# Seven block products for eight in the two feed-forward matrices of a decoder trunk, on one core

## The chip, the core and the metric

The kernel runs on one core of a Trainium2 chip. The metric is the device time of the whole program in microseconds, the median of the runs. Beside the runs there is one execution taken by the hardware profiler; all rows below are from it. The engines are TensorE (PE; its weight loads are listed as PEld), VectorE (DVE), ScalarE (ACT), GpSimd (POOL) and SyncE (SP), which issues every DMA here.

## What is computed

Two layers of a decoder trunk on 1024 tokens of width 1024, all in float32. A layer is a token mixer (attention heads and state-space groups behind a common projection, then an output projection), a layer norm, and a feed-forward block of width 4096 with a squared ReLU, with another layer norm behind it:

```python
h = layer_norm(DEEPNORM_ALPHA * h + mix_out, ln1_g[l], ln1_b[l])
ff = jnp.square(jax.nn.relu(h @ w_ff1[l] + b_ff1[l])) @ w_ff2[l] + b_ff2[l]
h = layer_norm(DEEPNORM_ALPHA * h + ff, ln2_g[l], ln2_b[l])
```

## The kernel before, in words

**Precision.** A float32 matrix is split into a high and a low part, `hi` by a rounding copy on ScalarE and `lo = x - hi` by a subtraction (`split`, L205 to 207, normally on VectorE). A block product is then three matrix products, hi·hi, hi·lo and lo·hi, added up in PSUM. A matrix product (`mm`, L203) has a 128x128 stationary operand and 512 columns.

**Order of work.** The program is written as Python generators which are stepped in turn (`run`, from L1172); each step issues some instructions. A scheduler then sorts the instructions of every engine by the order of the program and by the time at which it reckons that they can start. Every engine, SyncE too, takes its own list strictly in order. SBUF is one pool of 50 pages of 128 x 4 KB (`Pages`, L96; a part set aside is a `Ring`, L118); a page is taken from the front of the free list, and who takes it waits until its last reader is done. PSUM has eight banks under five names (`mm` 2, `a` 2, `b` 2, `c` 1, `s` 1).

**Feed-forward.** The hidden width is cut into 16 chunks of 256, the tokens into two halves of 512. `ff1(c, h)` (L1059) computes 256 hidden columns of one half, transposed: for each of two blocks of 128, 24 products into one bank, then ReLU with bias and a square on ScalarE, a square on VectorE and the subtraction that gives the low part. `ff2(cs, tiles)` (L1079) multiplies a chunk with its 256 rows of the second matrix: for each token tile of 128 and each of two column halves 6 products, then VectorE adds the bank to the residual page `r[i]`. `ff_load` (L1046) loads the weights of a chunk (512 KB a page) and splits them. The activations never leave SBUF. `ff_ahead` (L1104) takes chunks on the first token half from the time on at which that half is through its first layer norm, while the output projection (`gen_out`, L926), the layer norm (`ln_tiles`, L972) and the transposes (`ln_turn`, L1020) of the second half go on. `ffn` (L1120) does the rest: one `ff1` unit and one `ff2` unit in turn, the last two chunks together, token tile by token tile (event 3), so that the layer norm of a tile (`done`) follows as soon as it is complete.

**Beside it.** In layer 0 the tables of the state space of layer 1 (`gen_tables`, L464, `ssm_tables`, L395) are made during `ffn`, one step of them behind each event, 25 steps: the preparation (L294), and for each of eight units three steps with a ring of three pages. A unit has four products of 512 elements and a memset on GpSimd, nine operations of 512 elements on VectorE, some small matrix products, and stores 1.5 MB. The layer norm's scale and bias are two GpSimd operations of 1024 elements for each token tile (L991, L992).

## Time and profile before

| | |
|---|---|
| median of 3 runs | 2573.41 us (2568.72 to 2579.18) |
| profiled execution, span from first to last instruction | 2578.3 us |
| TensorE busy | 2387.0 us, 93% |
| VectorE busy | 1686.2 us, 65% |
| ScalarE busy | 895.4 us, 35% |
| GpSimd busy | 672.9 us, 26% |
| DMA | 297.24 MB, 115 GB/s over the span |

The profiled execution has no time of its own beside its span; the span lies inside the range of the three runs. "Busy" of TensorE counts overlapping matrix products once. In a list of groups "xN" is the number of instructions and "mean ns of one" the time of one alone; matrix products overlap, so that one that takes 390 ns alone starts every 226 ns. Layer 0's feed-forward lies at about 520 to 1360 us of the span, layer 1's at 1780 to the end.

### The profile page before, as it was taken

The numbers are of one execution on the slowest core, as the hardware profiler recorded it, in microseconds if no ns is written. First come the engines' busy times: TensorE is split into PE (matmuls) and PEld (weight loads), VectorE is DVE, ScalarE is ACT, GpSimd is POOL, SyncE is SP. The second block draws the span as 40 slices with busy tenths as digits, with TensorE's granted clock in tenths as the row PEclk, the third lists the DMA queues.
The fourth block names the chain that finished last, engine by engine and source line by source line (L and its number), as shares of the span: only waits on it lengthen the run. The fifth ranks groups of instructions, "written<-read, shape, count | busy, mean of one in ns | idle before, by whom it ended". The sixth has DMA issues, their size and how long they took to land.

```text
span 2578.3 us, 30595 instructions
## 1 busy us (share of the span) xinstructions
PE 2387.0 (93%) x11200; PEld 1951.8 (76%) x11200; DVE 1686.2 (65%) x2967; ACT 895.4 (35%) x1416; POOL 672.9 (26%) x537
## 2 busy tenths in 40 slices
PE   8988787879999999999999998896999999999995
PEld 7766675657788888888878786784778888888884
DVE  8686687876676666545584667789685545454548
ACT  4444566341332322222232544745232212121221
POOL 3465566141111111000152546624030000000004
PEclk9998898979999999999999999997999999999998
DMA  6588873332232322212145768532322212121201
GB/s 217 203 276 250 225 193 102 102 114 74 66 99 92 119 79 86 85 47 76 36 128 182 237 198 253 159 91 90 121 67 66 82 33 66 33 66 33 82 17 66
DMA packets 156471, 297.24 MB, mean 115 GB/s; under 512 B 55456, under 2 KB 74016, under 8 KB 156320
## 3 DMA queue, kind: packets, MB, share of 16 engines
q1 hardware_dynamic: 156320, 295.29, 37.0%
q8 instruction: 88, 1.44, 0.2%
q14 instruction: 63, 0.52, 0.1%
HBM read 228.90 MB, written 63.96 MB: 114 GB/s over the span
## 4 chain that ended last, share of the span: by engine, by line
PE 66%; DVE 13%; DMA 7%; issue 3%; ACT 2%; POOL 1%; SPq 1%; DVEq 0%; ACTq 0%; POOLq 0%
PE ps_mm L203 37%; PE ps_a L203 12%; PE ps_b L203 11%; PE ps_s L203 2%; DMA vr<-vD 2%; DVE wl L188 2%; PE ps_c L203 2%; DMA K<-qk 1%; PE ps_b L764 1%; SPq L185 1%; DVE hT L188 1%; POOL qt L188 1%; DVE S L740 1%; DVE CY L506 1%; DMA wr<-in_w_in_dram 1%
## 5 line engine op out<-in xcount | busy, mean ns | idle before, releaser
L203 PE MATMUL ps_mm<-hT,wh 128*128 128x512 f32 x2816 | 892.6, 396 | 21.5 <-DVE qt L678 11.1
L203 PEld LDWEIGHTS ps_mm<-hT,wh 128*128 128x128 f32 x2816 | 531.4, 190 | 135.6 <-DVE qt L678 9.0
L203 PE MATMUL ps_mm<-hT,wl 128*128 128x512 f32 x1408 | 554.5, 394 | 0.3 <-DVE wl L188 0.3
L200 ACT ACTIVATE wh<-wr 128x1024 fp32r<-128x1024 f32 (+1 forms) x233 | 241.6, 1051 | 458.3 <-PE ps_a L203 257.1
L188 DVE TENSOR_TENSOR wl<-wr,wh 128x1024 fp32r<-128x1024 f32 (+1 forms) x233 | 312.8, 1354 | 105.2 <-ACT wh L200 104.8
L203 PEld LDWEIGHTS ps_mm<-hT,wl 128*128 128x128 f32 x1408 | 268.0, 190 | 56.7 <-DVE wl L188 0.7
L200 ACT ACTIVATE rl<-ps_mm,cols 128x512 f32<-128x512 f32 x128 | 88.1, 688 | 599.4 <-PE ps_mm L203 596.6
L203 PE MATMUL ps_a<-wh,H 128*128 128x512 f32 x928 | 288.1, 391 | 1.6 <-DVE r L188 1.6
L203 PE MATMUL ps_b<-wh,H 128*128 128x512 f32 x928 | 286.6, 389 | 0.0
L188 DVE TENSOR_TENSOR rl<-rl 128x512 f32<-128x512 f32 x128 | 108.5, 848 | 267.9 <-ACT rl L200 267.9
L188 DVE TENSOR_TENSOR r<-ps_a,r 128x512 f32<-128x512 f32 x216 | 148.6, 689 | 140.0 <-PE ps_a L203 140.0
L188 DVE TENSOR_TENSOR r<-ps_b,r 128x512 f32<-128x512 f32 x216 | 146.4, 687 | 100.6 <-PE ps_b L203 99.1
L203 PEld LDWEIGHTS ps_a<-wh,H 128*128 128x128 f32 x928 | 173.1, 188 | 38.5 <-DVE r L188 2.0
L203 PEld LDWEIGHTS ps_b<-wh,H 128*128 128x128 f32 x928 | 174.2, 188 | 36.2
L203 PE MATMUL ps_mm<-wh,ms 128*128 128x512 f32 x512 | 166.0, 406 | 19.4 <-ACT wh L200 17.0
L188 POOL TENSOR_TENSOR xm<-xm,AG 128x1024 f32<-128x1024 f32 x7 | 16.7, 2391 | 633.1 <-ACT xm L200 633.1
L188 POOL TENSOR_TENSOR r<-xh,AG 128x1024 f32<-128x1024 f32 x24 | 67.1, 2815 | 439.5 <-DVE xh L194 439.5
L203 PE MATMUL ps_a<-wl,H 128*128 128x512 f32 x464 | 180.8, 390 | 0.0
L203 PE MATMUL ps_b<-wl,H 128*128 128x512 f32 x464 | 180.7, 389 | 0.0
L194 POOL TENSOR_SCALAR S<-S,mn 128x384 f32<-128x384 f32 (+7 forms) x128 | 105.7, 829 | 137.9 <-DVE mn L743 82.8
L203 PEld LDWEIGHTS ps_mm<-wh,ms 128*128 128x128 f32 x512 | 96.7, 194 | 42.1 <-ACT wh L200 17.5
L200 ACT ACTIVATE S<-S,mn 128x384 f32<-128x384 f32 (+7 forms) x128 | 98.8, 772 | 78.1 <-DVE mn L740 71.4
(260 smaller groups left out, 3803.0 us busy)
## 6 DMA issues: line engine op xcount, KB each, us to landing
wr<-in_w_ff_dram SPq DMA_DIRECT2D x152, 512.0 KB
wr<-in_w_in_dram SPq DMA_DIRECT2D x40, 512.0 KB
cs<-cs SPq DMA_DIRECT2D x32, 512.0 KB
LV<-LV SPq DMA_DIRECT2D x32, 512.0 KB
DL<-DL SPq DMA_DIRECT2D x32, 512.0 KB
qk<-q SPq DMA_DIRECT2D x32, 512.0 KB
wr<-in_w_out_dram SPq DMA_DIRECT2D x32, 512.0 KB
K<-qk SPq DMA_DIRECT2D x64, 256.0 KB
```

Source lines behind the costliest of these rows:

```text
L185: return self.nc.sync.dma_start(out=out, in_=in_)
L188: (eng or self.nc.vector).tensor_tensor(out, x, y, op)
L194: (eng or self.nc.vector).tensor_scalar(out, x, s0, s1, op0, op1)
L200: self.nc.scalar.activation(out, x, f, **k)
L203: self.nc.tensor.matmul(out, lhsT, rhs, start=start, stop=stop, **k)
L506: nc.vector.tensor_tensor_scan(C[:, g], s["rho"][:, g0 + g:g0 + g + 1].to_broadcast([P, P]), A[:, g], 0.0, OP.mult, OP.add)
L740: nc.vector.tensor_tensor_reduce(pp[:, c0:c1], ps[:, :c1 - c0], self.mask[:, m0 + c0:m0 + c1], -0.125, mn[:, 0:1] if n else 3e38, OP.add, ...
L764: nc.tensor.transpose(pt[:, base:base + P], PP[i][:, P * j:P * j + P], self.ident)
```

## The change

Both matrices of the feed-forward are cut into quadrants and multiplied in Winograd's form of Strassen's scheme: seven block products for eight, with sums of the quadrants of both operands ahead of them (S1 to S4 on the activations, T1 to T4 on the weights) and sums of the products behind. The first matrix is done in two phases. Phase A (`gen_ffa`) has the two products of the first token half and runs where `ff_ahead` ran; what it gives (product M1 and the finished quadrant H11) goes to DRAM. Phase B (`gen_ffb`) has the other five; it computes the sums of the weights on GpSimd, finishes the hidden quadrants, forms the sums S1 to S4 for the second matrix, and stores six pieces of 128x512 per chunk. `gen_ff2` loads those and the weights back, takes the first 14 chunks in pairs with seven products for a pair, and adds the seven sums at the end. The last two chunks are multiplied as before (`ff2_tail`). The residual pages go to DRAM behind the first layer norm and come back ahead of the second matrix; the first half's activations `x` go to DRAM too and come back for the sums (`gen_sums`). The tables of layer 1 are stepped by phase B, one step at each of its two yields a chunk, and the rest behind it.

The parts of the diff that matter (`split` is as before; `pair_split` splits a page into two pages, `one_split` half a page into one):

```diff
- "kmax": 2,
+ "kmax": 6,
+ "fbw": 13, "fbt": 8, "f2r": 14, "f2o": 20,
...
+    def gen_sums(self, X):
...
+        for j in range(2):
+            a21, a22, a11, a12 = X[j], X[2 + j], Z[j], Z[2 + j]
+            s1 = pg.get((2, 512), name="xs")
+            self.tt(s1, a21, a22, OP.add)
+            F["S1"].append(self.pair_split(s1))
+            yield
+            self.tt(a21, a11, a21, OP.subtract, eng=gp)
+            F["S3"].append(self.pair_split(a21))
+            yield
+            self.tt(a11, s1, a11, OP.subtract)
+            F["S2"].append(self.pair_split(a11))
+            yield
+            pg.free(s1, a21)
+            F["A22"].append(self.pair_split(a22))
+            yield
+            self.tt(a12, a12, a11, OP.subtract, eng=gp)
+            F["S4"].append(self.pair_split(a12))
+            yield
...
+    def quad(self, ps, B, A, start, stop):
+        bh, bl = B
+        n = 0
+        for k in range(4):
+            ah, al = (z[:, k % 2] for z in A[k // 2])
+            for w, x in ((bh, ah), (bh, al), (bl, ah)):
+                self.mm(ps, w[:, k], x, start and n == 0, stop and n == 11, skip_group_check=True)
+                n += 1
...
+    def gen_ffa(self):
...
+        for c in range(n):
+            nxt = start(c + 1) if c + 1 < n else None
+            yield
+            t, ps = cur
+            w = W.pop(c)
+            self.quad(ps, [z[:, 4:8] for z in w], F["A12"], False, True)
+            ring.free(*w)
+            load(c + 2)
+            self.act(t[:, 1], ps, AF.Relu, bias=self.hbias(2 * c))
+            self.act(t[:, 1], t[:, 1], AF.Square)
...
+            self.dma(d, t)
...
+    def gen_ffb(self):
...
+        wr, tr = Ring(pg, PRM["fbw"]), Ring(pg, PRM["fbt"])
...
+        def prep(c):
+            m0, m1 = (wr.get((KD, P), name="wr") for _ in range(2))
+            self.dma(m0, a["w_ff1"][l, 2 * c])
+            self.dma(m1, a["w_ff1"][l, 2 * c + 1])
+            u, v = (wr.get((KD, P), name="wt") for _ in range(2))
...
+            self.tt(T1, B12, B11, OP.subtract, eng=gp)
+            self.tt(T3, B22, B12, OP.subtract, eng=gp)
+            x = self.pair_split(u, shape=(KD, P), pg=wr)
+            self.tt(T2, B22, T1, OP.subtract, eng=gp)
+            wr.free(u)
+            self.tt(T4, T2, B21, OP.subtract, eng=gp)
+            wr.free(m0)
+            y = self.pair_split(v, shape=(KD, P), pg=wr)
+            wr.free(v)
+            z = self.one_split(B22, shape=(2, 4, P), pg=wr)
...
+            p5 = self.psum(("mm", "a")[c % 2])
+            self.quad(p5, first(x), F["S1"], True, False)
+            self.act(M5, p5, AF.Copy)
+            p6 = self.psum("b")
+            self.quad(p6, first(y), F["S2"], True, False)
+            self.tt(U2, p6, M1, OP.add)
+            self.quad(p5, [z[:, 0], z[:, 1]], F["S4"], False, True)
...
+            self.tt(A12, p5, U2, OP.add)
+            self.relu_square(A12, self.hbias(2 * c + 1))
+            yield
+            self.quad(p6, last(x), F["S3"], False, True)
...
+            self.tt(U3, p6, M1, OP.add)
+            self.tt(A22, U3, M5, OP.add, eng=gp)
...
+            self.quad(p4, last(y), F["A22"], True, True)
...
+            self.tt(A21, U3, p4, OP.subtract)
+            self.relu_square(A21, self.hbias(2 * c))
...
+                self.tt(S1, A21, A22, OP.add)
+                self.tt(S3, H11, A21, OP.subtract)
+                self.dma(d[:, 1:3], u)
+                self.tt(S2, S1, H11, OP.subtract)
+                self.tt(S4, A12, S2, OP.subtract)
+                self.dma(d[:, 3:5], v)
+                self.dma(d[:, 0], A12)
+                self.dma(d[:, 5], A22)
...
+    def gen_ff2(self, r):
...
+        R, O = Ring(pg, PRM["f2r"]), Ring(pg, PRM["f2o"])
...
+            if g == 0:
+                G[0, c] = take(p0, gp, True), take(page(((0, ah[:, 1]), (1, hq[:, 0]))))
+            elif g == 1:
...
+                self.tt(u[:, 0], B12, B11, OP.subtract, eng=gp)
+                self.tt(u[:, 1], B22, B12, OP.subtract, eng=gp)
+                G[1, c] = take(u, gp, True), take(s)
+            else:
...
+                self.tt(v[:, 0], B22, u[:, 0], OP.subtract, eng=gp)
+                R.free(u)
+                self.tt(v[:, 1], v[:, 0], B21, OP.subtract, eng=gp)
...
+                b22 = self.one_split(B22, pg=O)
...
+                a22 = self.one_split(x[:, 0], pg=O)
...
+                G[2, c] = take(v, gp), take(s), b22, a22
...
+        def product(i, ops, fresh):
+            nonlocal turn
+            for t in range(4):
+                ps = self.psum(tags[turn % 2][t])
+                o = slice(P * t, P * t + P)
+                for q, ((ah, al), (bh, bl)) in enumerate(ops):
+                    for j, (x, w) in enumerate(((ah, bh), (ah, bl), (al, bh))):
+                        self.mm(ps, x[:, o], w, q == 0 and j == 0, q == len(ops) - 1 and j == 2)
+                at = place[i](t)
+                if fresh and i in (1, 6, 7):
+                    self.act(at, ps, AF.Copy)
+                else:
+                    self.tt(at, at, ps, OP.subtract if i == 4 else OP.add)
+            turn += 1
...
+        for t in range(4):
+            eng = gp if t % 2 else None
+            rt, rb, u2, u3 = r[t], r[4 + t], U[t][:, 1], place[7](t)
+            self.tt(rt[:, 0:512], rt[:, 0:512], U[t][:, 0], OP.add, eng=eng)
+            self.tt(u2, u2, U[t][:, 0], OP.add, eng=eng)
+            self.tt(rt[:, 512:1024], rt[:, 512:1024], rb[:, 512:1024], OP.add, eng=eng)
+            self.tt(rt[:, 512:1024], rt[:, 512:1024], u2, OP.add, eng=eng)
+            self.tt(u3, u3, u2, OP.add, eng=eng)
+            for c in (0, 512):
+                self.tt(rb[:, c:c + 512], rb[:, c:c + 512], u3, OP.add, eng=eng)
...
+            sums = self.gen_sums(X.pop(1))
+            for _ in sums:
+                next(side, None)
+            for _ in side:
+                pass
...
-            self.ffn(done, bg, final)
+            for _ in self.gen_ffb():
+                next(bg, None)
+            for _ in bg:
+                pass
+            for i in range(NT):
+                r[i] = pg.get(name="r")
+                self.dma(r[i], rS[i])
+            for _ in self.gen_ff2(r):
+                pass
+            final()
+            if not last:
+                self.wring = Ring(pg, 12)
+                self.proj_load()
+            for i in range(NT):
+                self.ff2_tail(i, r)
+                done(i)
```

In `gen_ff2` the products of a pair run in the order 1, 2, 5, 7, 6, 4, 3. `prep(1)` is issued ahead of product 1, `prep(2)` and the loads of the next pair ahead of product 5, `prep(0)` of the next pair ahead of product 6. U holds products 1 and 6, Y product 7; the others are added to `r` at once.

## Rows read from the trace of the kernel before

**Rows 1.** The page: span, and busy time of each engine
```profile
span 2578.3 us, 30595 instructions
PE 2387.0 (93%) x11200; PEld 1951.8 (76%) x11200; DVE 1686.2 (65%) x2967; ACT 895.4 (35%) x1416; POOL 672.9 (26%) x537
```

**Rows 2.** Busy time of each engine by stretch, granted clock, DMA
```profile
core 0: us, PE busy (x) PEld busy (x) DVE busy (x) ACT busy (x) POOL busy (x), PEclk, DMA share, GB/s
...
700.00:800.00 100.00, 100.00 (x445) 82.80 (x444) 72.85 (x160) 30.97 (x43) 14.88 (x22) 1.00 0.29 95
...
1500.00:1600.00 100.00, 90.11 (x492) 75.78 (x492) 71.02 (x145) 44.36 (x83) 60.14 (x55) 0.95 0.78 236
1600.00:1700.00 100.00, 90.23 (x481) 72.40 (x480) 81.13 (x186) 64.54 (x110) 56.73 (x53) 0.95 0.56 155
...
2200.00:2300.00 100.00, 100.00 (x443) 82.85 (x442) 46.70 (x64) 19.49 (x26) 0.00 (x0) 1.00 0.14 43
...
690.00:1300.00 610.00, 610.00 (x2784) 500.75 (x2783) 365.89 (x569) 156.99 (x230) 61.99 (x60) 1.00 0.25 81
```

**Rows 3.** Groups by line and form: TensorE, products with hT
```profile
L203 PE MATMUL ps_mm<-hT,wh 128*128 128x512 f32 x2816 | 892.6, 396 | 21.5 <-DVE qt L678 11.1 <-DVE r L197 4.0 <-DVE hT L188 3.1
L203 PE MATMUL ps_mm<-hT,wl 128*128 128x512 f32 x1408 | 554.5, 394 | 0.3 <-DVE wl L188 0.3
```

**Rows 4.** Timeline of VectorE at three places: start, duration, operation, count
```profile
520.71 7.40 DVE L188 TENSOR_TENSOR hT<-ht,hT 128x512 fp32r<-128x512 f32 x3 [3.24 <-ACT hT L200]
...
753.61 1.22 DVE L188 TENSOR_TENSOR wl<-wr,wh 128x1024 fp32r<-128x1024 f32 x1
754.74 0.28 DVE L188 TENSOR_TENSOR scr<-scr 128x128 f32<-128x128 f32 x1
...
756.95 0.68 DVE L188 TENSOR_TENSOR rl<-rl 128x512 f32<-128x512 f32 x1
757.55 0.68 DVE L188 TENSOR_TENSOR bst<-bst,tp 128x512 f32<-128x512 f32 x1
...
770.30 0.43 DVE L194 TENSOR_SCALAR cs<-wk 128x512 f32<-128x512 f32 x1
770.64 0.68 DVE L188 TENSOR_TENSOR r<-ps_a,r 128x512 f32<-128x512 f32 x1
```

**Rows 5.** Timeline of GpSimd beside the first of those places
```profile
519.65 2.34 POOL L188 TENSOR_TENSOR r<-r,AB 128x1024 f32<-128x1024 f32 x1
521.96 2.81 POOL L188 TENSOR_TENSOR r<-xh,AG 128x1024 f32<-128x1024 f32 x1
524.74 5.61 POOL L188 TENSOR_TENSOR r<-r,AB 128x1024 f32<-128x1024 f32 x2
```

**Rows 6.** One tile's operations: duration ns min/median/max, first and last start
```profile
L188 DVE TENSOR_TENSOR hT<-ht,hT x48: 670/681/2883, 520.7 to 1917.3; 128x512 fp32r<-128x512 f32 x48
...
L740 DVE CUSTOM_DVE_ANT_0 S<-ps_a,mask x128: 261/670/693, 156.6 to 1744.4; 128x512 f32<-128x512 f32 x80, 128x128 f32<-128x128 f32 x16, 128x256 f32<-128x256 f32 x16, 128x384 f32<-128x384 f32 x16
...
L188 POOL TENSOR_TENSOR AB<-AB x16: 1260/1286/1297, 239.8 to 1615.3; 128x512 f32<-128x512 f32 x16
```

**Rows 7.** The view of rows 2 for shorter stretches
```profile
500.00:670.00 170.00, 134.48 (x573) 106.60 (x573) 127.48 (x194) 56.67 (x76) 60.66 (x23) 0.89 0.24 78
...
550.00:560.00 10.00, 5.54 (x14) 4.43 (x15) 7.32 (x6) 4.01 (x4) 5.27 (x3) 0.52 0.64 210
1440.00:1450.00 10.00, 8.91 (x57) 6.94 (x56) 8.21 (x23) 4.33 (x11) 7.32 (x9) 1.00 0.94 333
```

**Rows 8.** The view of rows 3: ScalarE, a split of 1024 and a square of 512
```profile
L200 ACT ACTIVATE wh<-wr 128x1024 fp32r<-128x1024 f32 x231 | 240.3, 1055 | 456.3 <-PE ps_a L203 257.1 <-PE ps_mm L203 106.2 <-DMA wr<-in_w_ff_dram 40.9
...
L200 ACT ACTIVATE H<-rl 128x512 fp32r<-128x512 f32 x128 | 80.1, 627 | 1.8
```

**Rows 9.** Timeline of GpSimd: one product of the tables
```profile
765.75 1.10 POOL L188 TENSOR_TENSOR wk<-pw,bst 128x512 f32<-128x512 f32 x1
```

**Rows 10.** Who waited for whom: us in total, times, longest
```profile
POOL wk L188 <- DMA DL<-DL: 116.1, 6, 25.0
```

More of the change, by code (lines that the diff above doesn't have):

```diff
@@ L1038, in ln_turn @@
         pg.free(*XH)
-    def ff_begin(self, l, hT, r):
-        n = DFF // 256
-        self.F = dict(l=l, hT=hT, r=r, W={}, H={}, sums=None, next=False, last=n - 1, K=0,
-                      need=[(w, c) for c in range(n - 2) for w in (1, 2)])
-    def ff_load(self, lim=99):
-        F, ring, a = self.F, self.wring, self.a
-        while F["need"] and F["need"][0][1] <= lim and len(ring.free_list) >= 4:
-            w, c = F["need"].pop(0)
-            src, shape = (a["w_ff1"], (KD, P)) if w == 1 else (a["w_ff2"], (D,))
-            F["W"][w, c] = [self.load_w(src[F["l"], 2 * c + m], shape, pg=ring) for m in range(2)]
-        if not F["need"] and F["next"]:
-            self.proj_load()
@@ new lines, in pair_split, with one_split, x_turn @@
+    def pair_split(self, src, eng=None, shape=(2, 512), pg=None):
+        pg = pg or self.pg
+        hi, lo = (pg.get(shape, F32R, name="sp") for _ in range(2))
+        self.split(hi, lo, src, eng)
+        return hi, lo
+    def one_split(self, src, eng=None, shape=(2, 512), pg=None):
+        t = (pg or self.pg).get(shape, F32R, name="sh")
+        self.split(t[:, 0], t[:, 1], src, eng)
+        return t
+    def x_turn(self, h, XH, gcol, bcol, l, tags=("b",)):
+        pg = self.pg
+        cols = self.cols[l]
+        out = []
+        for k in range(KD):
+            pt = self.psum(tags[k % len(tags)])
+            for q in range(4):
+                self.nc.tensor.transpose(pt[:, q * P:q * P + P], XH[q][:, P * k:P * k + P], self.ident)
+            if k % 2 == 0:
+                out.append(pg.get((2, 512), name="xt"))
+            self.act(out[-1][:, k % 2], pt, AF.Identity, scale=cols[:, gcol + k:gcol + k + 1],
+                     bias=cols[:, bcol + k:bcol + k + 1])
+        pg.free(*XH)
+        return out
@@ new lines, in ff_begin @@
+    def ff_begin(self, l, X):
+        pg = self.pg
+        F = self.F = dict(l=l, n=DFF // 256, K=0, ah=[], hq=[], sums=None)
+        F["xD"] = []
+        A = []
+        for x in X:
+            d = self.dram.tile([P, 2, 512], F32, tag=f"xd{len(A)}", name=f"xd{len(A)}_{self.uid()}")
+            self.dma(d, x)
+            F["xD"].append(d)
+            A.append(self.pair_split(x))
+            pg.free(x)
+        F["A11"], F["A12"] = A[:2], A[2:]
+    def gen_sums(self, X):
+        pg, F = self.pg, self.F
+        gp = self.nc.gpsimd
+        Z = []
+        for d in F["xD"]:
+            z = pg.get((2, 512), name="xz")
+            self.dma(z, d)
+            Z.append(z)
+        for n in ("S1", "S2", "S3", "S4", "A22"):
+            F[n] = []
+        for j in range(2):
[16 more added lines that the diff above has]
+            yield
+            pg.free(a22, a11, a12)
@@ new lines, in ff2_tail @@
+    def ff2_tail(self, i, r):
+        F = self.F
+        o = slice((i % 4) * P, (i % 4) * P + P)
+        for n in range(2):
+            ns = slice(512 * n, 512 * n + 512)
+            ps = self.psum("ab"[(i + n) % 2])
+            q = 0
+            for W, X in F["tail"]:
+                (bh, bl), (ah, al) = W[n], X[i // 4]
+                for m in range(2):
+                    for x, w in ((ah, bh), (ah, bl), (al, bh)):
+                        self.mm(ps, x[:, m, o], w[:, m], q == 0, q == 11)
+                        q += 1
+            self.tt(r[i][:, ns], ps, r[i][:, ns], OP.add)
+            sums = F["sums"]
+            if sums is not None:
+                if n == 0:
+                    sums[i] = self.small("fst", [2, 6], bufs=4)
+                self.nc.vector.bn_stats(sums[i][:, n], r[i][:, ns])
+        if i % 4 == 3:
+            for _, X in F["tail"]:
+                self.pg.free(*X[i // 4])
+        if i == NT - 1:
+            for W, _ in F["tail"]:
+                for w in W:
+                    self.pg.free(*w)
@@ L1227, in run @@
             self.F = None
-            hT1 = [[None, None] for _ in range(KD)]
+            X = {}
+            rS = [self.dram.tile([P, D], F32, tag=f"rs{i}", name=f"rS{i}_{l}") for i in range(NT)]
             def gen_side():
@@ L1257, in gen_side @@
                 self.wring = Ring(pg, 8)
[L1258 to L1259 removed]
+                self.ff_begin(l, X.pop(0))
+                yield from self.gen_ffa()
             def out_ssm(h):
@@ L1321, in run @@
                     next(side, None)
-            while "F" not in st and self.F is None:
+            while self.F is None:
                 next(side)
@@ L1352, in run @@
                 self.proj_begin(l + 1, items(l + 1))
-                self.F["next"] = True
                 def final():
```

299 lines of the change are left out of this document (183 added, 116 removed).

## The prediction

> **What bounds the kernel now.** I read the page's first two parts first, then the busy time by 100 us stretches, then the groups of instructions, and last the timeline of VectorE and GpSimd where they work together. TensorE is busy 93% of a span of 2578.3 us [rows 1]. The windows tell where the other 7% lies: in the feed-forward stretches (690 to 1300 us in layer 0; 2200 to 2300 stands for layer 1) it is busy without a gap at the full clock of 2.4 GHz; in the latter 443 products of 128x512 start, so 100/443 = 0.2257 us each [rows 2]; in the mixer stretches VectorE and GpSimd are both at 55 to 80% and TensorE at 90% [rows 2]. So the feed-forward is bound by the number of matrix products and by nothing else, and a product removed there is worth 0.2257 us, as long as the other engines keep up with what replaces it. That is the question of this case. In that last stretch GpSimd does nothing and VectorE works 47% of the time [rows 2].
>
> **What is removed.** Before, a chunk of 256 hidden columns takes 2x2x24 = 96 products in the first matrix and 8x2x6 = 96 in the second; 16 chunks and 2 layers make 6144. The trace has them: 4224 products of hT, of which 1152 are the projections' q, k and u (48 outputs of 24), leave 3072 [rows 3]; the second matrix has as many. After, the first matrix takes 24 in phase A and 60 in phase B, 84 in a chunk. The second takes 7 products x 24 for each pair of chunks times 7 pairs, and the last two chunks stay as they were (192): 1368 for 1536. So 192 + 168 = 360 products a layer go, 720 in all: **-162.5 us**. Nothing else on TensorE changes by more than a few products.
>
> **What the other engines get.** Prices, from start to start where the trace has two in a row: VectorE 0.60 us for 512 elements and 1.13 for 1024 [rows 4]; GpSimd 1.27 for 512 and 2.34 for 1024 when left alone [rows 5, 6].
>
> The rows that speak against the change are those where both work. While GpSimd ran four 1024-element sums back to back, three VectorE operations on 512 elements took 7.40 us instead of 1.8, and the sums 2.81 instead of 2.34 [rows 4, 5]: one goes, then the other, 2.80 us for a couple that would need 2.34 + 0.60 = 2.94 strictly in turn. The same form ranges from 670 to 2883 ns; an operation with one operand in PSUM never passes 693 ns in 128, all of them in the attention, where GpSimd is busy [rows 6]. The evictions of the new kernel are of that kind. So two engines share something that VectorE needs only for two SBUF operands, and I add up both engines' times on it. The Trainium skill (SBUF — State Buffer, "SBUF: two separate sides") calls this an exclusive lock held for the whole instruction, against VectorE operations with two SBUF inputs; the trace agrees in kind, and in size it shows 5% of overlap where the page allows none. By the page, layer 0's phase B below would come to 276 us instead of 265, and the sum to 11 us more.
>
> *Phase A* (24 products, 5.4 us a chunk): one split of 1024 on ScalarE and VectorE, three 512 activations. No bound. Its 384 products (87 us) fill the stretch in which the second half's output projection, layer norm and operand sums go on; before, chunks of the first half did this. Both kernels start it at the end of attention. The stretch has 35.5 us of idle TensorE now (134.5 busy of 170, 500 to 670 us), with holes like the one at 550 to 560 [rows 7]. The change takes two VectorE operations per output off it and adds the sums: 14 VectorE operations of 1024 (16 us) and 4 of GpSimd (9.4 us) that share the port, 25 us, behind the last transpose. Fill and chain are about equally long (130 to 140 us each), so something shows: **+12 us** for both layers, bounds -20 (all VectorE relief is gained) and +50 (all of the sums are exposed).
>
> *Phase B* (60 products, 13.5 us a chunk). VectorE: two lo splits of 1024 and one of 512, four evictions, four sums: 7.7 us. GpSimd: five sums, 6.35 us. Shared: 5.3 + 6.35 = 11.6 of 13.5 us. ScalarE: two splits near 1 us, one half, a copy, six activations near 0.6 [rows 8]: about 7. DMA: 1.5 MB in, 1.5 MB out, 3.15 MB in 13.5 us = 233 GB/s; the trace moves 333 GB/s at 94% of the DMA engines [rows 7], so it fits. The raw pages are free as soon as the chunk before is split, so loads go a chunk ahead. Layer 1: VectorE at about 72% with its waits, GpSimd at 47%. The nearest rows are 700 to 800 us (73% and 15%: TensorE 100%) and 1500 to 1600 (71% and 60%: 90%) [rows 2]; I take 96%, **+9 us** (0 to +22).
>
> In layer 0 the state-space tables of layer 1 run beside it, one step at each of phase B's yields, so eight units over some 12 chunks. A unit is four GpSimd products near 1.1 us [rows 9] and nine VectorE operations, seven of 0.60 and two scalar ones of 0.34 [rows 4]: 4.9 us. Shared time of the whole phase: GpSimd 16x6.35 + 8x4.4 + 6 = 143, VectorE 16x5.3 + 8x4.9 + 9 = 133 (the 6 and 9 are my allowance for the preparation, whose operations are small): 276 us, times 2.80/2.94 for the overlap = 265. TensorE has 16x13.5, and with an allowance of 9 for the tables' small products 225. So **+40 us**. Lower bound 0 (table work slips into gaps and off the chain); upper +91 (VectorE's 173 us of work there plus a wait for each of GpSimd's operations, 143, is 316). I stand at the shared time since the rows show a strict alternation.
>
> *Second matrix* (168 products, 37.9 us a pair). VectorE: 28 evictions (16.8), six lo splits of 1024, four of 512: 26.0 us. GpSimd: six lo splits of weights (2.35) and eight sums (1.27): 24.3. Shared: 9.2 + 24.3 = 33.5 of 37.9. With GpSimd at work 64% of the time a VectorE operation that needs the port waits some 0.6 us, ten of them 6 us: VectorE at 32 of 37.9, 85%. The nearest row is 1600 to 1700 us (81% and 57%): TensorE 90% [rows 2]. There attention's chains add waits that are not here; the operands here come two products ahead. I take 95.5%: 12 us a layer, **+24** (0 to +77, the second rival).
>
> *Phase B to the second matrix.* The splits of the first pair need pages that chunk 15 holds until its result is stored: after the last product an eviction 0.7, two activations 1.2, a store of 0.79 MB (2.4 at the 333 GB/s of rows 7), then the split on ScalarE 1.0 and GpSimd 2.35: 8 us idle. After such a hole the trace shows the clock at 0.52, the lower of its two levels (1.2 GHz), and 14 products in 5.5 us instead of 3.2 [rows 7]: 3 us more. Twice 11: **+22** (0 to +40). The eight r pages are reloaded on pages long free; first needed by product 2's eviction.
>
> *Second matrix to the last two chunks.* Seven sums for each of four tiles, half on VectorE (14x0.60), half on GpSimd (14x1.27) in strict dependence, before r can take the last evictions. r[0]'s seven take 4.2 us alone and 13 in turn with GpSimd's (7 x 1.87); r[3] is done after 18 us alone, 26 in turn; TensorE can run two tiles (10.8 us) ahead and reaches the fourth after 16. I take 8 a layer, **+16** (0 to +36). The last eight pages of operands (4.2 MB, 12.6 us at 333 GB/s) are loaded during the last three products (16.3 us).
>
> *SP's queue.* All new transfers (ah, hq, rS, xd) stand in one order with the loads. In phase B chunk c's last store waits for S4, some 3 us into the next chunk, and behind it stand the loads for chunk c+2, which have a whole chunk (13.5 us) until they are split: nothing, as long as no store is later than that.
>
> **Sum:** -162.5 + 12 + 9 + 40 + 24 + 22 + 16 = -39.5 us on the profiled 2578.3, which lies 4.9 us above the median of 2573.4 and inside the three runs' 2568.7 to 2579.2. From the median: 2573.4 - 39.5 = 2534; I say **2535**.
>
> **Rivals.** *All hidden.* If table work and waits fit in gaps, only the boundaries cost: -162.5 + 12 + 22 + 16 = -112, 2461. For it: on VectorE alone every phase is under 90%. Against: both stretches of rows 2 with GpSimd above 55% have TensorE at 90%.
>
> *The shared port decides everywhere (slower).* If each of the ten VectorE operations waits for a whole GpSimd operation (24.3/14 = 1.74 us), a pair takes 26.0 + 17.4 = 43.4 us: +5.5 x 14 = +77; layer 0's phase B +91. Sum -162.5 + 77 + 91 + 9 + 12 + 22 + 16 = +64, 2638. It decides from a mean wait of (37.9 - 26.0)/10 = 1.2 us on. For it: 2.5 us per operation in rows 4. Against: there GpSimd's queue never ran dry.
>
> *Tables hold GpSimd's queue.* They have three pages; now GpSimd waits up to 25 us for a table's store, 116 us in six waits [rows 10], which costs nothing since nothing is behind it. In phase B the next chunk's weight sums are behind it. If each of eight units blocks 5 us beyond the shared time, layer 0 loses 40 more: no change, 2574. Against: the scheduler reckons with a page's wait when it orders the queue.
>
> That the products are not removed is excluded by the counts above.
>
> **How the numbers follow.** Forecast 0.47 (2500 to 2560), all hidden 0.18, tables' queue 0.12, port everywhere 0.23. A change within 0.5% (2560.5 to 2586.3) is about what the measurement can't tell from none. Faster: 0.18 + nearly all of 0.47 = 0.63; same: the queue's 0.12 and 0.02 of the forecast's edge = 0.14; slower 0.23. These chances have both signs, so the likeliest's own range is 2500 to 2560; the range for 8 in 10 takes the better half of each far rival: 2452 to 2625.
>
> **What would show it.** 10480 instructions on TensorE for 11200. In layer 0's phase B (some 265 us) VectorE's two-SBUF operations at 1 to 3 us and TensorE near 85%; in layer 1's TensorE near 96%; in the second matrix 39 to 40 us a pair; an idle of 5 to 10 us at its start, with the low clock behind. Wrong if TensorE idles for DMA in phase B, if the pair takes over 42 us, or if layer 0's phase B is as quick as layer 1's.

## The result and the profile after

| | before | after |
|---|---|---|
| median (lowest to highest), 4 runs each | 2575.0 us (2568.7 to 2579.2) | 2602.2 us (2596.9 to 2607.8) |
| profiled execution, span | 2578.3 us | 2595.1 us (2596.9 as a run) |

The ratio is 1.0112, with an interval of 1.0089 to 1.0134: the change makes the kernel 1.1% slower, where 1.5% faster was forecast. The time lies inside the range of 2452 to 2625, on the slower side, which had a chance of 0.23.

The page of the kernel after, for [rows 1]:

```profile
span 2595.1 us, 31080 instructions
...
PE 2278.6 (88%) x10480; PEld 1835.9 (71%) x10480; DVE 1926.1 (74%) x3035; ACT 1125.5 (43%) x1716; POOL 1392.6 (54%) x937
```

The 720 products are gone. TensorE is busy 108 us less, yet the span is 17 us longer: TensorE now idles where it did not. The busy time by stage shows where; columns as in [rows 2] (layer 0: phase B, hand-over to the second matrix, second matrix; then the same for layer 1, and its end):

```profile
700.00:960.00 260.00, 232.47 (x1017) 181.75 (x1016) 220.15 (x303) 126.80 (x200) 152.65 (x119) 0.96 0.67 231
960.00:1045.00 85.00, 42.58 (x187) 31.97 (x186) 37.23 (x37) 27.30 (x43) 41.45 (x28) 0.72 0.51 180
...
1045.00:1285.00 240.00, 236.30 (x1037) 194.13 (x1037) 204.07 (x236) 91.84 (x107) 177.36 (x87) 1.00 0.46 150
1990.00:2220.00 230.00, 218.04 (x926) 176.07 (x924) 136.40 (x161) 104.99 (x154) 107.43 (x76) 0.98 0.66 228
2220.00:2245.00 25.00, 12.49 (x44) 9.54 (x44) 11.35 (x10) 12.63 (x16) 24.61 (x14) 0.80 0.78 267
2247.00:2500.00 253.00, 252.54 (x1113) 208.45 (x1112) 213.77 (x246) 97.02 (x115) 178.05 (x88) 1.00 0.43 136
2500.00:2595.00 95.00, 57.07 (x223) 44.15 (x221) 86.94 (x172) 11.66 (x10) 49.68 (x25) 0.83 0.14 55
```

In words, stage by stage. The second matrix runs almost without a gap in both layers, with VectorE at 85%; in layer 1 it takes 253/1113 = 0.2273 us a product, 38.2 us a pair. Phase B loses a little in layer 1 and more in layer 0. The hand-over of layer 0 is the surprise: 42 of 85 us idle, the clock at 0.72 in the mean, and no other engine is half busy either.

What those engines wait for is seen in GpSimd's and TensorE's timelines there (start, duration, idle before and its releaser):

```profile
992.87 1.04 POOL L189 TENSOR_TENSOR wk<-cst,fh 128x512 f32<-128x512 f32 x1
...
1008.71 1.10 POOL L189 TENSOR_TENSOR DL<-pw,spc 128x512 f32<-128x512 f32 x1 [0.18 <-DMA cs<-cs]
...
1022.84 1.04 POOL L189 TENSOR_TENSOR wk<-cst,fh 128x512 f32<-128x512 f32 x1 [12.57 <-DMA DL<-DL]
...
1033.66 1.10 POOL L189 TENSOR_TENSOR DL<-pw,spc 128x512 f32<-128x512 f32 x1 [8.72 <-DMA cs<-cs]
```

```profile
1010.59 0.56 PE L204 MATMUL ps_s<-DL,bst 128*16 128x112 f32 x2 [5.61 <-DVE DL L189]
...
1026.75 1.09 PE L436 MATMUL ps_s<-cst,wk 128*128 128x128 f32 x4 [14.32 <-DVE wk L189]
...
1035.54 0.55 PE L204 MATMUL ps_s<-DL,bst 128*16 128x112 f32 x2 [6.23 <-DVE DL L189]
...
1037.31 2.62 PE L204 MATMUL ps_b<-sp,sp 128*128 128x512 f32 x6
```

These are the last two units of the tables of layer 1. GpSimd waits for the store of a table page (DL, cs) before it may write the next one, as in [rows 10]; the small products of those units stand in TensorE's list ahead of the second matrix, and TensorE waits 26 us for them in the first three lines shown. Another 13 us are waits for the first pair's operands, as in layer 1 (5.8 us until 976 us, 7.5 until 987). In the kernel before, the first GpSimd operation of the eight units (first and last start at the end of the line) is this:

```profile
L188 POOL TENSOR_TENSOR wk<-cst,fh x8: 1039/1040/1528, 764.8 to 1023.4; 128x512 f32<-128x512 f32 x8
```

The last unit began at the same time, 1023 us, but there 340 us of feed-forward were still to come.

Where the time went, by stage: the loss of a stage is TensorE's idle time plus its busy time times what the granted clock lacks of full speed, added up over windows of 5 us. "Measured" is the loss after minus the loss before, rounded.

| stage, both layers unless said | forecast | measured |
|---|---|---|
| mixers and phase A | +12 | -2 |
| phase B, layer 0 | +40 | +36 |
| phase B, layer 1 | +9 | +16 |
| phase B to second matrix, layer 0 | +11 | +50 |
| phase B to second matrix, layer 1 | +11 | +16 |
| second matrix | +24 | +4 |
| its sums and the end of the layer | +16 | +38 |
| TensorE's busy time at the granted clock | -162.5 | -141.5 |
| sum | -39.5 | +16.8 |

### The profile page after: what moved, and what is told of

The parts are those of the page before. It is cut to its first block, busy times and chain, and to the rows that moved or that the text cites. A ratio compares the mean times of both kernels' runs of the same rounds, so it can differ in the third digit from the quotient of the medians.

```text
span 2595.1 us, 31080 instructions
## 1 busy us (share of the span) xinstructions
PE 2278.6 (88%) x10480; PEld 1835.9 (71%) x10480; DVE 1926.1 (74%) x3035; ACT 1125.5 (43%) x1716; POOL 1392.6 (54%) x937
## 5 line engine op out<-in xcount | busy, mean ns | idle before, releaser
L204 PE MATMUL ps_b<-sp,sp 128*128 128x512 f32 x1368 | 345.9, 400 | 23.1 <-DVE tu L189 9.7
L204 PEld LDWEIGHTS ps_b<-sp,sp 128*128 128x128 f32 x1368 | 261.2, 193 | 88.1 <-DVE tu L189 13.3
L204 PE MATMUL ps_a<-sp,sp 128*128 128x512 f32 x1008 | 257.1, 403 | 20.9 <-DVE r L189 12.4
L204 PE MATMUL ps_mm<-hT,wh 128*128 128x512 f32 x768 | 249.8, 403 | 9.9 <-DVE qt L679 8.1
L204 PEld LDWEIGHTS ps_a<-sp,sp 128*128 128x128 f32 x1008 | 195.6, 195 | 67.1 <-DVE r L189 15.0
L204 PE MATMUL ps_mm<-sp,sp 128*128 128x512 f32 x816 | 206.1, 398 | 33.1 <-ACT sp L201 16.1
L204 PEld LDWEIGHTS ps_mm<-sp,sp 128*128 128x128 f32 x816 | 155.2, 192 | 70.9 <-ACT sp L201 18.4
L204 PE MATMUL ps_mm<-sp,wh 128*128 128x512 f32 x512 | 175.5, 426 | 22.9 <-ACT mh L201 10.7
L204 PEld LDWEIGHTS ps_mm<-hT,wh 128*128 128x128 f32 x768 | 144.9, 192 | 42.0 <-DVE qt L679 8.2
L204 PE MATMUL ps_mm<-hT,wl 128*128 128x512 f32 x384 | 153.1, 399 | 0.9 <-DVE wl L189 0.9
```

The source lines that it names most:

```text
L204: self.nc.tensor.matmul(out, lhsT, rhs, start=start, stop=stop, **k)
```

## The experiments

Times are medians against the kernel before on the same chip (2574.9 to 2576.3 in the five comparisons); the changed kernel's is 2602.2. "Phase B" is the time from the first chunk's copy of M5 (the product of S1 and T1, which ScalarE copies out of PSUM) to the last's, 15 chunks, whose 900 products alone take 900 x 0.2257 = 203.1 us; "layer 0's rest" is from there to the last split of the layer's output. These come from one profiled execution each; the runs of one kernel lie up to 18 us apart, so a difference of a few us between two kernels tells nothing by itself.

**Runs 1 and 2: without layer 1's tables.**

```diff
-                bg = self.gen_tables(l + 1, 3)
+                bg = iter(())
+                self.sp[l + 1] = self.sp[l]
```

> The changed kernel without the tables of layer 1 (layer 1 reads layer 0's tables, so its output is that of other state-space parameters; the work of reading and using them is the same). Theory: the tables are what turns layer 0: they share GpSimd, VectorE and TensorE's queue with phase B, and their last units run alone behind it. Then phase B of layer 0 becomes like that of layer 1 (idle and slow-clock loss 44 to about 18 us) and the 42 us hole at its end becomes like the 14 us of layer 1: 54 us less, about 2548. Rival: phase B and the hand-over cost this by themselves (weights, stores, page reuse): at most 15 us less, 2587 or more.

> The kernel before without the tables of layer 1. Theory: there they lie wholly under TensorE's products, so it stays within 5 us of the 2575 of before. Rival: they cost the old kernel something too, 15 us or more less; then what the first run shows is not the change's alone.

Measured: 2524.3 us, 78 less than the changed kernel, and 2563.1, 12.7 less than before. So the tables cost 65 us more beside the new feed-forward than beside the old, and without them the change is worth 2563.1 - 2524.3 = 39 us. The tile that takes M5 shows phase B, in the changed kernel's layer 0:

```profile
L201 ACT ACTIVATE tu<-ps_a x8: 575/590/599, 702.4 to 958.4; 128x512 f32<-128x512 f32 x8
L201 ACT ACTIVATE tu<-ps_mm x8: 575/582/601, 705.7 to 939.7; 128x512 f32<-128x512 f32 x8
```

and in run 1's:

```profile
L201 ACT ACTIVATE tu<-ps_a x8: 573/577/588, 706.9 to 925.9; 128x512 f32<-128x512 f32 x8
```

Phase B goes from 256.0 to 219.0 us, and layer 0's rest from 452 to 411: 37 and 42 us. Layer 1's phase B takes 221.4 in the changed kernel, so without tables the two layers are alike. The first theory stood in kind: phase B and the hand-over become like those of layer 1, though the gain is 78 for its 54. Of the second pair neither number holds: 12.7 us is more than the theory's 5 and less than the rival's 15.

**Run 3: the new feed-forward in layer 1 only.** `ff_ahead` and `ffn` of before serve layer 0.

> Layer 0 with the old feed-forward, layer 1 with the new one. Theory: the two layers can be added up from the two traces. Layer 0 ends 47 us earlier than in the changed kernel, layer 1 takes 1184 us for 1214: 2575 - 30 = 2545 to 2550, faster than both. Rival: the 20 us that layer 1's mixer lost less in the changed kernel come from the way in which layer 0 ended there and go with it: about 2568, no change.

Measured: 2550.9 us, ratio 0.9915 (0.9900 to 0.9931). The layers add up, as in the theory: layer 1 alone gains 24 us, and the loss is layer 0's.

**Runs 4 and 10: GpSimd's work moved to VectorE**, that of phase B's weight sums, and that of the tables.

```diff
-            self.tt(T1, B12, B11, OP.subtract, eng=gp)
+            self.tt(T1, B12, B11, OP.subtract)
```

```diff
-        gp = nc.gpsimd
+        gp = nc.gpsimd if s["layer"] == 0 else nc.vector
```

(The first is done for T1 to T4, the second stands in `ssm_tables`.)

> The changed kernel with T1 to T4 of phase B on VectorE in place of GpSimd. Theory (shared port): a chunk's shared time falls from 11.6 to 9.0 us, phase B's loss in layer 0 from 44 to about 25 and in layer 1 from 18 to about 9, and GpSimd is freer for the tables: 25 to 35 us less, about 2572. Rival (VectorE's own time is what counts): it has 10.1 of a chunk's 13.5 us, in layer 0 with the tables about 12.5, and its queue is longer ahead of the evictions: 10 to 30 us more, about 2620.

> The changed kernel with the GpSimd products and memset of layer 1's tables on VectorE (four of 0.60 us a unit for four of 1.1). Theory: the tables are dear because GpSimd and VectorE take turns at the shared port and hand each other the chain: phase B of layer 0 loses 15 us or more less, about 2570 to 2585. Rival: they are dear because each engine takes its list in order and the tables' steps, which wait for one another, stand in all of them: within 10 us of 2602, or slower.

Measured: 2584.3 (18 less: the sign of the theory, not its size) and 2620.2 (18 more, as in the rival). In layer 1, where no tables run, phase B of the changed kernel and of run 4:

```profile
L201 ACT ACTIVATE tu<-ps_mm x8: 573/578/598, 1993.5 to 2198.6; 128x512 f32<-128x512 f32 x8
L201 ACT ACTIVATE tu<-ps_a x8: 574/578/598, 1998.5 to 2214.9; 128x512 f32<-128x512 f32 x8
```

```profile
L201 ACT ACTIVATE tu<-ps_mm x8: 576/578/600, 2006.3 to 2194.2; 128x512 f32<-128x512 f32 x8
L201 ACT ACTIVATE tu<-ps_a x8: 577/579/600, 2017.2 to 2209.1; 128x512 f32<-128x512 f32 x8
```

221.4 us become 202.8, the bare products: what phase B loses in layer 1 comes from the four sums a chunk being on GpSimd, though VectorE has 2.4 us more work for them. That this is the shared port is not shown. The move also takes the sums off a slower engine, and the waits in the changed kernel's phase B of layer 1 (us in total, times, longest) point there:

```profile
POOL wt L189 <- DMA wr<-in_w_ff_dram: 88.9, 13, 9.9
ACT sp L201 <- POOL wt L189: 41.8, 16, 5.2
PE ps_mm L204 <- ACT tu L201: 5.9, 3, 2.9
```

One such chain, from three engines' timelines:

```profile
2112.30 1.28 POOL L189 TENSOR_TENSOR wt<-wr,wr 128x512 f32<-128x512 f32 x1 [8.18 <-DMA wr<-in_w_ff_dram]
...
2116.17 2.14 POOL L189 TENSOR_TENSOR wt<-wt,wr 128x512 f32<-128x512 f32 x1
...
2118.35 1.06 ACT L201 ACTIVATE sp<-wt 128x1024 fp32r<-128x1024 f32 x1 [1.81 <-POOL wt L189]
...
2119.83 0.58 ACT L201 ACTIVATE tu<-ps_mm 128x512 f32<-128x512 f32 x1
...
2120.46 4.60 PE L204 MATMUL ps_mm<-sp,sh 128*128 128x512 f32 x12 [2.71 <-ACT tu L201]
```

GpSimd waits for the weights and then takes 6.0 us for the four sums, ScalarE's split waits for the last of them, the copy of M5 stands behind that split in ScalarE's list, and TensorE waits for the copy. VectorE is busy only 136.4 of 230 us there. In run 4 TensorE is busy throughout this stretch, 207.0 of 207 us. In layer 0 phase B is 241.7 us for 256.0, so 39 us above the bare products stay, and the rest is 9 us longer. Run 10 says that the tables' part on GpSimd is not dear by itself: with it on VectorE phase B is 2 us shorter and the rest 18 longer. But it gives VectorE four operations of 0.60 us a unit, so it does not separate port, list and VectorE's own time. Why VectorE can take the weight sums and not the tables was not tried further.

**Run 5: other pages for r.** In layer 0 the pages that the tables give back go behind the others in the free list.

```diff
+                N = [p for p in pg.free_list if p not in self.tabp]
+                N = N[:23] + N[27:] + N[23:27]
+                pg.free_list = N[:35] + self.tabp + N[35:]
```

> The changed kernel with another order of the free pages in layer 0 ahead of the second matrix: the residual pages r are no longer those that the tables give back last; these go to the end of the operand ring, which needs them two products later. Theory: SyncE takes its list in order and stands at the load of r for the tables' last unit, and with it the second matrix: the hole of 42 us at its start shrinks to some 15, so 20 to 30 us less, about 2577. Rival: TensorE's own list has the last units' small products in it and waits for their chain: within 6 us of 2602.

Measured: 2611.5 us, ratio 1.0144 (1.0118 to 1.0170). The loads of r moved as meant, from 954 to 1051 us to 946 to 963 us, and the hole stayed. The theory fell: r was one of those that waited, not what held the others. The rival's cause fits (TensorE again waits 14.3 us for one of the tables' products), but its "within 6 us" does not: the run is 9 us slower, and why is open.

**Run 11: the tables without TensorE's part, and run 14: without VectorE's.**

> The changed kernel with layer 1's tables without their 160 transposes and small products on TensorE (ScalarE copies SBUF data in their place, so the tables hold other numbers). Without the tables at all the kernel before lost 13 us, the changed one 78. Theory: of the 65 us between, most comes from TensorE's list, in which the tables' products wait for their chain while phase B's stand behind: 45 us less or more, about 2555. Rival: TensorE only lacks operands, since VectorE, ScalarE and GpSimd are held by the tables: 12 to 20 us less, about 2587.

> The changed kernel with layer 1's tables without their nine VectorE operations a unit (the tables hold other numbers; the preparation, GpSimd, ScalarE, TensorE and the transfers stay). Without TensorE's part it was 21 us less, with GpSimd's part on VectorE 18 us more. Theory: VectorE's list is what the tables hold in phase B (85 to 100% busy there, its waits at the port included): 40 to 60 us less, about 2552. Rival (the chain through ScalarE, the page ring and SyncE): 5 to 15 us less.

Measured: 2581.0 (21 less) and 2570.2 (32 less). Run 11 leaves phase B at 256.1 and takes 24 us off the rest, about the 26 that TensorE waited in its list; so that list is the hand-over's matter and not phase B's. It also shortens the tables' chain itself (a unit takes 37.5 us for the 42.8 shown below), so the 24 us are not the list's alone. Run 14 takes 46 us off the rest and adds 14 to phase B. Neither theory has its numbers: run 11 is 1 us beyond its rival's 12 to 20, run 14 lies between its two. I read this as a price shared by several lists.

**Run 7: five pages for the tables.** Two pages that hold raw weights elsewhere are idle then.

```diff
+        lent = list(self.raws.free_list) if l else []
+            ring.free_list += lent
```

> The changed kernel with five pages for the tables of layer 1 instead of three (two that no one uses at the time). Theory: their chain (compute, store, wait for the page) is what makes them late and holds the engines' lists; with two pages more two units overlap: the tables end inside phase B, the hole shrinks to 14 us as in layer 1 and phase B loses less than its 53 us: 35 to 55 us less, about 2557. Rival (they only take the shared port and TensorE's time): within 10 us of 2602.

**Run 13: the stores of cs and LV issued by ScalarE.**

> The changed kernel with the stores of two of the three table pages of a unit (cs and LV) issued by ScalarE, which writes them, and not by SyncE. Theory: in phase B of layer 0 SyncE stood 25 us for those pages (waits for ScalarE's cs 14.5, LV 5.8, VectorE's cs 5.2), with the weights and the M1/H11 loads of phase B behind: 15 to 30 us less, about 2580. Rival: the loads are a chunk ahead and do not feel it: within 6 us of 2602.

Measured: 2590.2 (12 less) and 2607.6 (5 more, inside its rival's 6, and some of its runs lie among the changed kernel's: SyncE's wait there costs nothing that shows). The first operation of the eight units, in the changed kernel and in run 7:

```profile
L189 POOL TENSOR_TENSOR wk<-cst,fh x8: 1036/1040/2052, 723.5 to 1022.8; 128x512 f32<-128x512 f32 x8
```

```profile
L189 POOL TENSOR_TENSOR wk<-cst,fh x8: 1033/1472/2760, 725.4 to 896.1; 128x512 f32<-128x512 f32 x8
```

A unit took 299.3/7 = 42.8 us with three pages and 24.4 with five, inside phase B. Then layer 0's rest is 412 us, that of run 1 without tables: the hole is gone, and it was the page ring that made it. But phase B is 282 us for 256: packed closer, the tables cost there 26 of the 40 us that they had cost behind, and the gain is 12 us for the 35 to 55 of the theory.

**Run 16: all parts together, both layers.** Weight sums on VectorE (but the first chunk's), five pages, and the edits of runs 9 and 13.

> Both layers new, with all that has helped: weight sums on VectorE, closing sums and last norm on VectorE, five pages for the tables, table stores from ScalarE. By addition 2602 - 18 - 16 - 12 = 2556, less what the thirteenth run gains. Theory: layer 0 stays dearer than with the old feed-forward, whose TensorE-bound stretch hides the tables: 20 to 40 us above the 2521 of the twelfth run. Rival (the tables were dear only through pages and lists): 2525 or less.

Measured: 2527.2 us, ratio 0.9809 (0.9791 to 0.9826), 29 below the sum of the parts. That is 6 us above run 12, where the theory asked for 20 to 40: the rival is nearer, and its 2525 is missed by 2. Phase B of layer 0 is 253 us and the rest 412: layer 0 ends at 1367 us for 1411. From the first copy of M5 to that end it takes 665 us for 708; run 7 alone takes 695, run 4 alone 703, runs 6 and 9 702. So the parts alone give 14, 6 and 7 us, 26 of the 43 (by the unrounded times). The other 17 come only when they are made together, above all, as I read it, pages and sums: each alone moves the tables' time to where the other limit holds.

**Runs 6 and 9: the end of the second matrix.** Run 6 does the closing sums on VectorE, the upper half first; run 9 also the last layer norm's two GpSimd operations.

```diff
-            self.tt(t, t, G, OP.mult, eng=nc.gpsimd)
-            self.tt(r[i], t, B, OP.add, eng=nc.gpsimd if i < NT - 2 else None)
+            self.tt(t, t, G, OP.mult)
+            self.tt(r[i], t, B, OP.add)
```

> The changed kernel with the closing sums of the second matrix all on VectorE, the upper token half's first, the lower half's behind. Theory (the sums contend for the shared port and hold r): the loss at the end of the second matrix falls from 30 and 41 us to about 15 and 30, so 20 to 25 us less in both layers, about 2580. Rival (the last operands' loads and the layer norm's chain set it): within 6 us of 2602.

> The kernel of the sixth run (closing sums on VectorE), and the two GpSimd operations of the last layer norm on VectorE too. Theory: behind the sums VectorE alone sets the end. In the sixth run TensorE ended 14 us earlier than in the changed kernel and the program only 5 us, because VectorE was busy from 2505 to 2590 us and its 128x1 operations of the layer norm waited 1.4 to 2.3 us each behind GpSimd's, about two for each token tile. Two operations of 1.13 us take the place of some 4 us of waits: 2 us for each of seven tiles, 10 to 15 us less than 2597, about 2585. Rival (VectorE's own work is the bound and grows by 2.3 us a tile): 2597 to 2610.

**Run 15: the same norm edit in the kernel before.**

> The kernel before with the two GpSimd operations of the last layer norm on VectorE, to see how much of the twelfth run's gain is not the change's. There TensorE ends 25 us before the program; if VectorE's waits behind GpSimd set that, 5 to 10 us less, about 2567; else 2575.

Measured: 2597.2 (5 less), 2585.9 (16 less), and 2563.7 for the kernel before, ratio 0.9956. TensorE's last products in the changed kernel and in run 6:

```profile
2565.92 3.01 PE L204 MATMUL ps_a<-sp,sp 128*128 128x512 f32 x12 [1.53 <-DVE r L189]
```

```profile
2552.05 2.88 PE L204 MATMUL ps_a<-sp,sp 128*128 128x512 f32 x12
```

Run 6's gain is the one that its rival has. TensorE ends 14 us earlier and the span at the same 2595 us: the sums did hold r, but behind them VectorE is next. (Some 4 of the 14 us were there at the end of phase B already.) VectorE's timeline in the changed kernel, and GpSimd's beside it, show why it is slow:

```profile
2551.37 2.35 DVE L198 SCALAR_TENSOR_TENSOR lfz<-lfz,fve 128x1 f32<-128x1 f32 x1
2553.75 0.16 DVE L198 SCALAR_TENSOR_TENSOR lfi<-lfz,lfi 128x1 f32<-128x1 f32 x1
2553.94 2.20 DVE L189 TENSOR_TENSOR lfz<-lfi 128x1 f32<-128x1 f32 x1
2556.17 0.16 DVE L198 SCALAR_TENSOR_TENSOR lfz<-lfz,fve 128x1 f32<-128x1 f32 x1
```

```profile
2551.31 2.39 POOL L189 TENSOR_TENSOR xm<-xm,AG 128x1024 f32<-128x1024 f32 x1 [2.08 <-DVE fst L1444]
...
2553.78 2.34 POOL L189 TENSOR_TENSOR r<-xm,AB 128x1024 f32<-128x1024 f32 x1
```

An operation on 128x1 that takes 0.16 us takes 2.35 when it starts with a GpSimd operation of 2.39, and both end together. Run 9 bears this out: 11 us less than run 6, where 10 to 15 were expected. That its median is 2586 for the 2585 expected is luck, since its five runs lie between 2582.6 and 2596.7, two of them among run 6's. Run 15's 11 us (5 to 10 were expected) are clear of noise: the interval of its ratio is 0.9941 to 0.9971.

**Runs 8, 12, 17 and 18: towards a better version.** Run 8 is run 3 with the weight sums on VectorE. Run 12 adds run 9's edits and leaves the first chunk's weight sums on GpSimd. Run 17 adds VectorE for the first pair's low parts and weight sums and for the last A22. Run 18 is run 16 with run 17's edit and without run 13's.

> Layer 0 with the old feed-forward, layer 1 with the new one and T1 to T4 on VectorE. Theory: in the fourth run layer 1's phase B went from 221 to 203 us for 15 chunks, no loss at all: 15 to 18 us less than the 2551 of layer 1 alone, about 2534. Rival: the first chunk's sums come later behind VectorE's own work (phase B began 10 us later there) and take most of it back: 2545 or more.

> The kernel of the eighth run (layer 1 only, weight sums on VectorE) with the first chunk's weight sums left on GpSimd, the closing sums on VectorE and the last layer norm on VectorE. By addition: 2530, less 8 (phase B starts as early as in the changed kernel), less 5 (sums), less 12 (norm): about 2505. If the norm's rival holds, 2515 to 2525.

> The twelfth run's kernel (layer 1 only), and in it, ahead of the second matrix, the first pair's weight sums and low parts (products 1, 2, 5, 7) and the last two chunks' A22 sum on VectorE. Theory: at that hand-over GpSimd is busy without a gap for 35 us and VectorE idles, and the last chunk's A22 stands 6 us behind weight work in GpSimd's list: the 27 us there shrink by 8 to 12, about 2512. Rival (the stores and loads through DRAM set it): 2518 or more.

> The sixteenth run's kernel (both layers) with the table stores back on SyncE and the same hand-over edit in both layers. By addition 2527 less 5 less two times 8 to 12: about 2502, and then below the seventeenth: with pages and lists mended the new feed-forward pays in layer 0 too. Rival: the tables keep layer 0 dearer, 2515 or more.

Measured: 2530.0, 2521.3, 2518.2 (ratio 0.9774, 0.9748 to 0.9799) and 2535.9. Run 8 comes out as in its theory (2534). Run 12 lies in the range given for a failed norm edit (2515 to 2525) but not for that reason: from the end of phase B to the end it is 10 us shorter than run 8, about the norm's part, and the 8 us that phase B was to start earlier are missing (its last copy of M5 is at 2148.9 us for 2149.6). Run 17, for which 2512 was expected, can't be told from run 12, and run 18 is not faster than run 16: the rival's 2515 or more, far from 2502. In run 18's hand-over of layer 0 TensorE does nothing for 20 us while the DMA engines are full (the last two columns); run 16's line for the same window is below it:

```profile
960.00:980.00 20.00, 0.00 (x0) 0.00 (x0) 6.17 (x7) 7.23 (x9) 2.53 (x2) 0.53 1.04 413
960.00:980.00 20.00, 9.56 (x36) 7.39 (x34) 6.85 (x7) 8.78 (x12) 13.38 (x9) 0.74 1.02 400
```

Transfers are as full in run 16, yet TensorE works there. What ends run 18's wait is a matter of VectorE's list too:

```profile
982.01 1.23 DVE L189 TENSOR_TENSOR sp<-wr,sp 128x1024 fp32r<-128x1024 f32 x1 [8.85 <-DMA hq<-th]
983.21 0.69 DVE L189 TENSOR_TENSOR tu<-ps_b,th 128x512 f32<-128x512 f32 x1
...
983.96 5.19 PE L204 MATMUL ps_b<-sp,sp 128*128 128x512 f32 x12 [25.92 <-DVE tu L189]
```

The low part of a weight, which run 17's edit put on VectorE, waits for a transfer there, and behind it stands an eviction of phase B's last chunk, for which TensorE waits. So at that place the transfers, as run 17's rival says, and the order of the list together make the hole. In layer 1 no run shows what holds the hand-over. The best version is that of runs 12 and 17: new feed-forward in layer 1 only, 2.1 to 2.3% faster than the kernel before. Of this the last norm's edit is not the change's: against run 15's 2563.7 the rest is 1.7% in run 12.

## Why the prediction was wrong, point by point

**What was right.** TensorE's 720 products fell as counted. Phase B of layer 0 was forecast at 265 us and took 256 x 16/15 = 273, TensorE busy 89% there (85% forecast), and 95% in layer 1 (96%). The nearness is in part luck. By the prediction's own factor 276 us become 263 and not 265 (and VectorE's 173 us of work in the upper bound are 171), and only six of the tables' eight units lay in phase B. Taking turns with no overlap, as the Trainium skill has it (SBUF — State Buffer, "SBUF: two separate sides"), gives 276 as an estimate; for the same reason these runs don't decide between the two.

**The step that failed** is the timing of the tables: "eight units over some 12 chunks". I took the place of their steps in the program for the time at which they run. From the row of before shown above, a unit took 258.6/7 = 37 us; eight are 296, more than the 265 that I gave to phase B. GpSimd's waits of [rows 10] are for the page ring, and run 7 shows for the changed kernel that the ring sets the pace. In place of 11 us the hand-over of layer 0 cost 50, some 34 more than layer 1's, which has no tables (run 7: it is the ring; run 11: TensorE's ordered list passes it on). This term alone, put right, would have made the sum -0.5 us, no change. That the kernel became slower takes the other terms: 55 us more in four of them and 38 less in three. The rival "tables hold GpSimd's queue" read [rows 10] rightly; it put the wait inside phase B, and "nothing is behind it" became untrue at another place and on another engine's list. That its price of 40 us is that of the 39 missed is luck.

**Terms mis-sized.** The sums and the end of the layers were 38 us for 16, 24 of them in layer 0 and 14 in layer 1. The sums hold r as I said, but I did not ask what is late next. In layer 1 it was VectorE with the last layer norm (runs 6 and 9). In layer 0, whose norm these runs leave as it is, VectorE has no pause while TensorE idles:

```profile
1295.00:1305.00 10.00, 7.57 (x30) 5.40 (x30) 10.00 (x10) 2.00 (x2) 5.10 (x3) 1.00 0.00 0
1305.00:1315.00 10.00, 5.83 (x19) 4.59 (x19) 10.00 (x12) 2.12 (x2) 8.36 (x5) 0.83 0.34 106
1315.00:1325.00 10.00, 7.02 (x25) 5.09 (x24) 10.00 (x12) 1.71 (x2) 3.91 (x3) 0.89 0.35 105
```

With all sums on VectorE (run 6) the loss there falls only from 30 to 26 us. Phase B of layer 1 was 16 for 9, the hand-over there 16 for 11. In that phase B I added up shared time; the trace has VectorE at 59% and not 72%, and GpSimd waits 88.9 us for weights that I had "a chunk ahead". In the other direction, the second matrix cost 4 for 24: a pair took 38.2 us and not 39 to 40, with VectorE at 85% as forecast. I read this as the merit of operands that come two products ahead; the rows of the attention that I took as nearest have chains that aren't here. The mixers with phase A cost nothing, for 12: some 5 us more in layer 0, some 6 less in layer 1. Whether relief and added sums cancel, as the term had it, no run shows.

**Not settled.** TensorE's busy time fell by 141.5 for 162.5. Products that start alone count for about 0.4 us and not 0.2257, and there are more of them in stretches with gaps; I did not place the 21 us more closely. Of the 65 us that the tables cost more, runs 7, 11 and 16 show the ring, TensorE's list and the closeness to GpSimd's sums; their shares depend on one another. Whether GpSimd's sums cost by the shared port or by their own pace is open.

**Rivals.** "All hidden" was right about the second matrix, and wrong at the boundaries and in phase B (52 us in both layers, where it had none). "Tables hold GpSimd's queue" came nearest to the time, 2574, and to the cause. "The shared port decides everywhere (slower)", 2638, is the one with the right sign, but not for its reason: the second matrix, on which it stood, is the one place where the port cost next to nothing.

## What to carry to other kernels

Background work that a long stage hides has a pace of its own, set here by its buffers: before a change shortens the stage, work out from the trace when the last piece starts and ends, and what stands behind it in every engine's ordered list. When a change has several limits in one place, removing one alone shows little; here edits that gave 26 us one by one gave 43 together. An edit that moves work to another engine changes its pace, its place in the lists and what it contends with, all at once, so look at the waits before you name the cause. And a change that pays in one layer and not in the other can be made in one.

## What the runs showed of the hardware

Two-operand VectorE operations on 128x1 are held by GpSimd as large ones are: 2.20 to 2.35 us for 0.16. I had looked for this on 512 and 1024 elements only. Evictions from PSUM are not held: in layer 1's second matrix, where GpSimd is busy 178 of 253 us, none takes more than 0.69 us, while operations with both operands in SBUF range up to 3.41 (minimum, median and maximum in ns):

```profile
L189 DVE TENSOR_TENSOR sp<-hr,sp x38: 1211/1472/3410, 2243.8 to 2487.4; 128x1024 fp32r<-128x1024 f32 x38
L189 DVE TENSOR_TENSOR r<-r,ps_b x26: 673/676/689, 2248.8 to 2479.8; 128x512 f32<-128x512 f32 x26
```

Moving two operations of 1.13 us to VectorE, which was busy 92% of the last 95 us of the changed kernel, made both kernels some 11 us shorter (run 9 against run 6, and run 15 against the kernel before).
